# A hybrid decoder layer on one core: three first loads on other queues, and two steps of the output phase moved by one

## The chip, the cores and the metric

The kernel runs on one core of a Trainium2 chip. The metric is the device time of one execution in microseconds; lower is better. A core has TensorE (matrix products; PE in the profile, with its weight loads as PEld), VectorE (DVE), ScalarE (ACT), GpSimd (POOL) and SyncE (SP), each working through its own instruction stream in order, and 16 DMA engines that move data between the memory off the core (HBM) and the core's own. A DMA is issued on the queue of an engine: SP's, ScalarE's or GpSimd's.

## The reference

One layer of a decoder on 256 tokens of width 2048, in float32. The input is normalised, multiplied with one wide matrix, and the columns feed two token mixers side by side: gated linear attention (branch a) and differential attention (branch b). Each branch has an output matrix, the two results are merged by gates, and a last matrix and norm give the output:

```python
h = rmsnorm(x, pre_norm_g[l])
proj = h @ w_in[l]
(a_q, a_k, a_v, a_g, a_lr, b_q, b_k, b_v, b_g, m_a, m_b) = jnp.split(proj, offsets, axis=-1)
...
y_a = o_a @ w_branch_a[l]
...
y_b = o_b @ w_branch_b[l]
merged = jax.nn.sigmoid(m_a) * y_a + jax.nn.sigmoid(m_b) * y_b
out = merged @ w_out[l]
x = x + rmsnorm(out, post_norm_g[l])
```

What matters here is the very first product, `h @ w_in`, which can begin when its first weights, the first part of x and the norm's gains are there; and the end of the chain, where `y_b` is computed in column groups of 512, each group is merged with its part of `y_a`, and the merged values go into `merged @ w_out`.

## The kernel before

**Splits.** Every float32 operand is split in two parts, hi and lo, and a product is the sum of hi x hi, hi x lo and lo x hi. A weight tile of 128 partitions is fetched in `load` (line 284) and split in halves in `emit_half` (line 313): ScalarE copies hi (line 345), VectorE subtracts to get lo (line 346). The hi and lo tiles and the raw tiles have three buffers each. `take` (line 354) hands a split half to the products and emits splits three halves ahead. The sequence of halves, `seq`, is worked out ahead of time, and loads and splits follow it.

**The start.** `preg_s`, the norm's gains (128x16), comes in on ScalarE's queue (line 371). x comes in as 16 blocks of 128x256, turned so that the model dimension lies on partitions: blocks 0 and 1 by the `load_x` of line 372, the others out of `load`, each group after the weight tile that the table `X_LOADS` names. `prep_x` (line 378) multiplies a block by its gain and splits it: hi on ScalarE (line 384), lo on VectorE (line 385). The first weight tile is loaded in two halves (`cuts` in line 294), and its first half is split in two pieces of 416 columns, where hi of the first piece is made by VectorE (line 340) and of the second by ScalarE (line 342). The products of this first stage are those of `first_joint` (lines 516 to 535; they show as L528). Up to then nine products on a tile of ones (line 432) keep TensorE busy.

**The late phase.** Two kinds of work alternate on TensorE, in an order written out by hand in the string `LATE_ORDER`: a point is one step of `late_plain` (line 443), a `p` one step of `half_set` (line 1401). A plain step (`half_tile`, 2.7 us by the profile) is one weight half against both token blocks; steps 0 to 7 are column group 2 of `y_b` ("y12"), steps 8 to 15 group 3 ("y13"), and then products of `w_out` follow. A `p` step is half of one of seven products of a scheme that gets the product of a 2x2 arrangement of blocks with seven multiplications rather than eight; they are taken in the order `LATE = (1, 5, 3, 6, 2, 7, 4)`, two halves each, first for the set "os0" of `w_out`'s columns, then for "os1". Their weights are the fetched blocks and sums of them, tiles `part_e`, `part_b` and `part_f`, formed by accumulating DMAs and by VectorE (line 282). `pinned[0]` is set, so the products stand in program order; the other engines' instructions are ordered by a planner.

After the eighth step of a column group `merged` (line 1324) adds its gate and branch a's part: four VectorE operations on 128x512 (lines 1330 and 1331, twice each), after which a task `turn(g)` is queued that transposes the merged values on TensorE (line 1313) and splits them for the product with `w_out`. `pump` lets such a task go one step after each plain step. The first merge belongs to column group 0, the third to group 2. `put_off` is a list that holds a function to be run later; an earlier phase uses it once and leaves it empty.

Of the kernel before, what the change touches and what calls it, by code (L numbers as in the profile page):

```python
# [36 lines left out]
PUT_OFF = 6  # L37
LATE = (1, 5, 3, 6, 2, 7, 4)
LATE_COLS = ((0, 512), (1536, 1024))
LATE_ORDER = "....." ".p.p.pp.p.pp.p.p.pp.p.pp" ".pp.pp.p.pp.p.p.pp.p.pp"  # L40
BRANCH_COLS = (512, 0)
BRANCH_ORDER = ".p.p.p.p.pp.pp.pp.p.p.p..p"
HALF_SETS = ("ys0", "os0", "os1")
# [67 lines left out]
def half_set_steps(name):  # L111

    steps = []
    for prod in LATE:
        r = {1: 0, 2: 2}.get(prod)
        steps += [("part", name, prod, h) if r is None else (name, r, h) for h in range(2)]
    return steps
# [10 lines left out]
def late_steps():  # L128
# [3 lines left out]
    parts = half_set_steps("os0") + half_set_steps("os1")  # L132
    return [(plain, parts)[n == "p"].pop(0) for n in LATE_ORDER]


@with_exitstack
def hybrid_kernel(ctx: ExitStack, tc, xt, xn, preg, postg, w, w2, gkb, glag, lamv, diffg, ident_d, causal_d, lmask_d, out):
    nc = tc.nc
    pe, act, dve, pool, sp = nc.tensor, nc.scalar, nc.vector, nc.gpsimd, nc.sync
# [12 lines left out]
    def u(shape, name, dtype=F32):  # L152
        count[0] += 1
        return big.tile(shape, dtype, tag="u", name=f"{name}_{count[0]}")
# [24 lines left out]
    def ps(tag):  # L179
        count[0] += 1  # L180
        return psum.tile([P, 512], F32, tag=tag, name=f"{tag}_{count[0]}")
# [28 lines left out]
    def weights(key, r):  # L210
        a, size = at[key][r]
        return w[a : a + P * size].rearrange("(p n) -> p n", p=P), size

    def link(s, name, t):
        count[0] += 1
        c = blocks.tile([P, 2048], F32, tag="chain", name=f"{name}_{count[0]}", bufs=4)
        (pool if s else sp).dma_start(c, weights(f"set{s}", {"a": 0, "b": 6}[name] + t)[0])
        chain[s, name, t] = c
# [65 lines left out]
    def load(j):  # L284
        key, r, h = seq[j]
        src, size = weights(key, r)
        n = size // 2
        early = key == "v0"
        if key == "v3" and r == 0:
            for i in range(2):  # L290
                link(0, "a", i)
        count[0] += 1
        raw = raws[key, r] = wpool.tile([P, 2048], F32, tag="raw", name=f"raw_{count[0]}")
        cuts = (0, n, size) if j in (0, 2) else (0, size)
        for a, b in zip(cuts, cuts[1:]):
            i = sp.dma_start(raw[:, a:b], src[:, a:b])
            if early or key[0] == "o" or key in ("y10", "y11", "y12", "y13", "ys0"):
                tc.keep_in_program_order(i)
        if early and j // 2 in X_LOADS:
            load_x(*X_LOADS[j // 2])  # L300
# [10 lines left out]
    loaded = [0]  # L311

    def emit_half():
# [3 lines left out]
        while loaded[0] < min(j + 2, len(seq)):  # L317
            if len(seq[loaded[0]]) == 3 and seq[loaded[0]][2] == 0:
                load(loaded[0])
            loaded[0] += 1  # L320
# [33 lines left out]
    def take(key):  # L354
        j = used[0]
        used[0] += 1
        while emitted[0] < min(j + 1 + AHEAD, len(seq)):
            emit_half()
        e, hi, lo = ready.pop(j)
        assert key in (e, e[0]), (e, key)  # L360
        return hi, lo
# [3 lines left out]
    preg_s = const.tile([P, KT], F32, name="preg_s")  # L365
    xraw = [u([P, 4, S], "xraw") for _ in range(4)]

    def load_x(kt, n, queue=sp):
        tc.keep_in_program_order(queue.dma_start(xraw[kt // 4][:, kt % 4 : kt % 4 + n, :], xt[:, kt : kt + n, :]))

    tc.keep_in_program_order(act.dma_start(preg_s, preg))
    load_x(0, 2)
    act.preload_act_table_set("natural_log_exp_and_others")

    def x_ops(kt):
# [167 lines left out]
    def half_tile(banks, n, q, ops, hi, lo, begin=0):  # L543
        for w, parts in ((hi, (0, 1)), (lo, (0,))):
            for j in range(2):
                kt = 2 * q + j
                a = ops(kt)
                for b in range(2):
                    for part in parts:
                        first, last = kt == begin and w is hi and part == 0, kt == KT - 1 and w is lo  # L550
                        i = mm(banks[b][:, :n], a[part][:, P * b : P * b + P], w[:, n * j : n * j + n], start=first, stop=last)
        latest[0] = i.ins

    def token_major(key, n, ops, step=1, upto=KT // 2):
        banks = [ps("mm"), ps("mm")]
        for q in range(upto):
            half_tile(banks, n, q, ops, *take(key))
            if q % 2 or not ts:
                pump(step)
            else:  # L560
                pump_eager()
        return banks
# [118 lines left out]
    put_off = []  # L681
# [563 lines left out]
    for g in range(4):  # L1245
        banks = token_major(f"ag{g}", 512, x_ops, LANES)
# [38 lines left out]
    for g in range(4):  # L1285
        parts_a.append(fetch(m0[g], "part", u))
        banks = token_major(f"y0{g}", 512, a_ops, LANES, 4 if g == 3 else 8)
# [14 lines left out]
    def turn(g):  # L1302
        for _ in range({0: 3}.get(g, 2)):
            yield
        copies = u2([P, 4, S], "copy") if g < 2 else None
        if g < 2:
            turned_f32.append(copies)
        for i in range(2):
            bank = ps("bg")
            for j in range(2):  # L1310
                for b in range(2):
                    c = P * (2 * i + j)
                    pe.transpose(bank[:, P * (2 * j + b) : P * (2 * j + b) + P], gb[g][:, b, c : c + P], ident)
            hi = mh[g][:, 2 * i : 2 * i + 2, :].rearrange("p a t -> p (a t)")
            lo = ml[g][:, 2 * i : 2 * i + 2, :].rearrange("p a t -> p (a t)")
            split_out(bank, hi, lo, 0.5)
            if g < 2:
                act.activation(copies[:, 2 * i : 2 * i + 2, :].rearrange("p a t -> p (a t)"), bank, AF.Copy, scale=0.5)
            yield
        done.add(("turn", g))  # L1320
# [3 lines left out]
    def merged(g, banks):  # L1324
        for b in range(2):
            t, src = gb[g][:, b, :], banks[b]
            if g < 2:
                src = ycell(b, g)
                dve.tensor_tensor(out=src, in0=banks[b], in1=src, op=ALU.add if 512 * g == BRANCH_COLS[0] else ALU.subtract)
            dve.scalar_tensor_tensor(out=t, in0=t, scalar=1.0, in1=src, op0=ALU.add, op1=ALU.mult)  # L1330
            dve.tensor_tensor(out=t, in0=t, in1=parts_a[g][:, b, :], op=ALU.add)
        tasks.append(turn(g))
# [3 lines left out]
    def ycell(b, g):  # L1336
        return yc[b][:, 512 * g : 512 * g + 512]
# [20 lines left out]
    def total(b, g, bank, i=None):  # L1358
        t = cell(b, g)
        tc.keep_in_program_order(dve.tensor_tensor(out=t, in0=bank, in1=t, op=ALU.add if left(g) else ALU.subtract))  # L1360
        if i is not None:
            square(b, t, 512, i)
            gain(b, t, 512 * g, 512)
        return t
# [78 lines left out]
    def late_plain():  # L1443
        for g in (2, 3):
            banks = [ps("mm"), ps("mm")]
            for q in range(8):
                half_tile(banks, 512, q, b_ops, *take(f"y1{g}"))
                if q == 7:
                    merged(g, banks)
                yield  # L1450
        pg.extend(u([P, 1024], "pg") for _ in range(2))
        for i in range(2):
            sp.dma_start(pg[i], postg[1024 * i : 1024 * i + 1024].partition_broadcast(P))
        pairs = [[ps("mm"), ps("mm")] for _ in range(2)]
        for r in range(2):
            for g in range(2):
                for h in range(2):
                    half_tile(pairs[g], 512, 4 + 2 * r + h, m_ops, *take(f"o{g}"), begin=8)
                    if r and h:
                        for b in range(2):  # L1460
                            total(b, g, pairs[g][b], g)
                    yield
# [37 lines left out]

    parts = (step for s in range(2) for step in half_set(f"os{s}", m_ops, late, cell, LATE_COLS[s]))
    plain = late_plain()
    pinned[0] = True
    for step in late_steps():
# [124 lines left out]
```

## Time and profile before

| | us |
|---|---|
| median of 3 runs | 1090.54 |
| lowest and highest | 1090.40 and 1091.04 |
| the profiled execution's own time | 1090.65 |
| its span in the profile | 1088.9 |
| granted TensorE clock, mean | 0.999 |
| TensorE's longest waits | 1.6 (before the products on ones), 1.0, 0.9, 0.4 |

The profile is that of one execution, and its span is from the first to the last instruction; 1.75 us of its time lie outside of the span. Times in the rows are counted from the span's start. A row of the timeline gives the start, the duration, the engine, the line, the operation with what it writes and reads, and in brackets the idle time of that engine before it and what ended that. SPq, ACTq and POOLq rows are DMAs being issued; landing is another matter, and the views by tile give it from the issue on. "L540" is the line of a helper through which nearly all products go, so rows are told apart by tile.

### The profile page before, as it was taken

What the parts mean: (1) busy time and instruction counts of PE and PEld (TensorE: products, weight loads), DVE (VectorE), ACT (ScalarE), POOL (GpSimd) and SP (SyncE); (2) the same over time, 40 slices, a digit from 0 to 9 for tenths busy, and PEclk for the clock granted to TensorE, in tenths of its full rate; (3) what the DMA queues carried; (4) which work ended last, traced back from release to release, by engine and by line L of the source; (5) the groups of instructions that cost most, each with busy time, mean ns of one, the idle gap of its engine ahead of it and who ended that gap; (6) DMA issues with size and microseconds to landing.
All of it is one profiled execution on the core that took longest, in us unless ns stands there. A gap on an engine that the chain in (4) does not pass through costs nothing.

```text
span 1088.9 us, 15341 instructions
## 1 busy us (share of the span) xinstructions
PE 1080.3 (99%) x5451; PEld 927.9 (85%) x5451; DVE 917.2 (84%) x1277; ACT 712.2 (65%) x1038; POOL 146.0 (13%) x217
## 2 busy tenths in 40 slices
PE   9999999999999999999999999999999999999997
PEld 8999888888888888888888888889888888888886
DVE  7887987978979889799797999658779867888896
ACT  7886766666666767667666655556777756565662
POOL 0201112021021211211221100020111011100000
PEclk9999999999999999999999999999999999999999
DMA  9889869689798796997986654598888769979752
GB/s 347 294 293 331 237 253 319 163 285 303 263 319 221 278 297 199 331 258 261 300 239 227 238 190 162 184 328 261 275 283 266 275 244 321 345 255 274 262 183 107
DMA packets 63757, 285.06 MB, mean 262 GB/s; under 512 B 8320, under 2 KB 11392, under 8 KB 45504
## 3 DMA queue, kind: packets, MB, share of 16 engines
q1 hardware_dynamic: 39808, 186.87, 48.8%
q0 software_dynamic: 23296, 96.48, 32.7%
q8 instruction: 43, 0.70, 0.2%
q10 hardware_dynamic: 576, 0.73, 0.2%
q14 instruction: 34, 0.28, 0.1%
HBM read 258.88 MB, written 25.17 MB: 261 GB/s over the span
## 4 chain that ended last, share of the span: by engine, by line
PE 98%; issue 1%; DMA 0%; DVE 0%; ACT 0%; POOL 0%; POOLq 0%; SPq 0%; ACTq 0%
PE mm L540 60%; PE bg L540 27%; PE mm L528 2%; PE bg L528 2%; PE mm L513 1%; PE bg L956 1%; PE bg L513 1%; PE bg L1121 0%; PE bg L1095 0%; DMA raw<-in_w_dram 0%; PE bg L1096 0%; PE bg L1133 0%; PE bg L1134 0%; PE bg L1132 0%; PE bg L1016 0%
## 5 line engine op out<-in xcount | busy, mean ns | idle before, releaser
L345 ACT ACTIVATE hi<-raw 128x1024 fp32r<-128x1024 f32 (+3 forms) x261 | 268.1, 1032 | 206.4 <-PE bg L540 103.9
L346 DVE TENSOR_TENSOR lo<-raw,hi 128x1024 fp32r<-128x1024 f32 (+3 forms) x263 | 311.6, 1189 | 87.8 <-ACT hi L345 84.3
L540 PE MATMUL mm<-hi,xs 128*128 128x512 f32 (+1 forms) x848 | 214.1, 386 | 0.0
L540 PEld LDWEIGHTS mm<-hi,xs 128*128 128x128 f32 x848 | 156.9, 188 | 25.9
L540 PE MATMUL bg<-xs,hi 128*128 128x512 f32 x640 | 164.8, 390 | 0.0
L346 DVE TENSOR_TENSOR lo<-a,hi 128x1024 fp32r<-128x1024 f32 x112 | 135.2, 1221 | 11.7 <-ACT hi L345 10.5
L540 PEld LDWEIGHTS bg<-xs,hi 128*128 128x128 f32 x640 | 120.3, 188 | 23.4
L345 ACT ACTIVATE hi<-a 128x1024 fp32r<-128x1024 f32 x112 | 118.6, 1060 | 30.8 <-PE mm L540 22.8
L540 PE MATMUL mm<-lo,xs 128*128 128x512 f32 (+1 forms) x424 | 117.7, 383 | 0.0
L540 PEld LDWEIGHTS bg<-xs,lo 128*128 128x128 f32 x640 | 87.3, 190 | 6.2
L540 PEld LDWEIGHTS mm<-lo,xs 128*128 128x128 f32 x424 | 79.5, 188 | 14.4
L540 PE MATMUL bg<-xs,lo 128*128 128x256 f32 x640 | 89.2, 282 | 0.0
L346 DVE TENSOR_TENSOR lo<-b,hi 128x1024 fp32r<-128x1024 f32 x56 | 67.5, 1224 | 7.8 <-ACT hi L345 6.8
L345 ACT ACTIVATE hi<-b 128x1024 fp32r<-128x1024 f32 x56 | 59.3, 1060 | 18.2 <-PE mm L540 15.8
L540 PE MATMUL mm<-hi,oah 128*128 128x512 f32 x128 | 50.9, 397 | 0.0
L540 PE MATMUL mm<-hi,oal 128*128 128x512 f32 x128 | 50.0, 391 | 0.0
L1107 ACT ACTIVATE prob<-prob,mx,score_scale 128x128 f32<-128x128 f32 x64 | 34.2, 537 | 10.7 <-DVE mx L1102 10.6
L240 POOL DMA_DIRECT2D b<-in_w_dram x28 | 24.4, 873 | 107.4 <-DVE a L248 103.4
L540 PE MATMUL mm<-hi,obh 128*128 128x512 f32 x96 | 37.7, 393 | 0.0
L540 PE MATMUL mm<-hi,obl 128*128 128x512 f32 x96 | 37.4, 390 | 0.0
L345 ACT ACTIVATE hi<-c 128x1024 fp32r<-128x1024 f32 x28 | 29.6, 1060 | 10.2 <-PE mm L540 5.3
L248 DVE TENSOR_TENSOR a<-a,b 128x1024 f32<-128x1024 f32 x28 | 34.1, 1223 | 0.4
(409 smaller groups left out, 2018.6 us busy)
## 6 DMA issues: line engine op xcount, KB each, us to landing
raw<-in_w_dram SPq DMA_DIRECT2D x114, 1024.0 KB, 6.1
a<-in_w_dram POOLq DMA_DIRECT2D x28, 512.0 KB, 13.6
c<-in_w_dram SPq DMA_DIRECT2D x28, 512.0 KB, 8.5
b<-in_w_dram POOLq DMA_DIRECT2D x28, 512.0 KB, 7.3
a<-in_w_dram POOLq DMA_DIRECT2D x12, 1024.0 KB, 5.3
b<-in_w_dram POOLq DMA_DIRECT2D x12, 1024.0 KB, 8.2
raw<-in_w_dram SPq DMA_DIRECT2D x14, 832.0 KB, 6.9
dh<-dh POOLq DMA_DIRECT2D x16, 256.0 KB, 4.7
```

Of the source, the lines that this page charges most:

```text
L240: pool.dma_start(chain[s, name, i][:, c], weights(f"set{s}", 2 + i)[0][:, c], accum_op=ALU.add)
L248: dve.tensor_tensor(out=a, in0=a, in1=chain[s, "b", i][:, c] if second else raws[s, i, h], op=ALU.add)
L345: act.activation(hi_t[:, a:b], r[:, a:b], AF.Copy)
L346: dve.tensor_tensor(out=lo_t[:, a:b], in0=r[:, a:b], in1=f32(hi_t[:, a:b]), op=ALU.subtract)
L513: i = pe.matmul(out, lhs, rhs, start=first and n == 0, stop=last and n == len(pairs) - 1, **kw)
L528: i = pe.matmul(banks[g][b][:, :n], a[part][:, P * b : P * b + P], w[:, n * g : n * g + n], start=first, stop=last)
L540: i = pe.matmul(*args, **kw)
L956: pe.matmul(o, xk[:, P * c : P * c + P], xq.rearrange("p (b c t) -> p b c t", b=2, c=4)[:, :, c, :], start=i == 0, stop=i == 1)
L1107: act.activation(prob[m][:, lo:up], prob[m][:, lo:up], AF.Exp, scale=score_scale[:, b : b + 1], bias=mx[:, i : i + 1], accum_out=z[:, i : ...
```

## The change

Four edits. The gains `preg_s` are loaded on GpSimd's queue. The first weight tile is loaded right behind the first blocks of x and ahead of the load of ScalarE's function table; its first half goes on ScalarE's queue, its second half, as all other weights, on SP's. In the late order the two halves of product 1 of "os0" each stand one plain step further ahead: before, the string read `......p.p.pp`, now `.....p.p..pp`, and from there on it is as it was. And the third merge, that of group 2, is not emitted after the last step of "y12" but kept in `put_off` and emitted after the first step of "y13", with its task `turn(2)`.

```diff
-LATE_ORDER = "....." ".p.p.pp.p.pp.p.p.pp.p.pp" ".pp.pp.p.pp.p.p.pp.p.pp"
+LATE_ORDER = ".....p.p..pp.p.pp.p.p.pp.p.pp" ".pp.pp.p.pp.p.p.pp.p.pp"
...
-            i = sp.dma_start(raw[:, a:b], src[:, a:b])
+            i = (sp if j or a else act).dma_start(raw[:, a:b], src[:, a:b])
...
-    tc.keep_in_program_order(act.dma_start(preg_s, preg))
+    tc.keep_in_program_order(pool.dma_start(preg_s, preg))
     load_x(0, 2)
+    load(0)
+    loaded[0] += 1
     act.preload_act_table_set("natural_log_exp_and_others")
...
                 half_tile(banks, 512, q, b_ops, *take(f"y1{g}"))
-                if q == 7:
+                if put_off and q == 0:
+                    put_off.pop()()
+                if q == 7 and g == 2:
+                    put_off.append(lambda banks=banks: merged(2, banks))
+                elif q == 7:
                     merged(g, banks)
                 yield
```

## The prediction

> **What bounds the kernel now.** I read the first page of the profile, then TensorE's waits over the whole span, then the two places where those waits fall: the first 6 us and the stretch around 984 us.
>
> ```profile
> span 1088.9 us, 15341 instructions
> PE 1080.3 (99%) x5451; PEld 927.9 (85%) x5451; DVE 917.2 (84%) x1277; ACT 712.2 (65%) x1038; POOL 146.0 (13%) x217
> PE 98%; issue 1%; DMA 0%; DVE 0%; ACT 0%; POOL 0%; POOLq 0%; SPq 0%; ACTq 0%
> PE bg L1567 <- ACT diag L1566: 1.0, 1, 1.0
> PE mm L528 <- ACT hi L342: 0.9, 1, 0.9
> PE bg L540 <- DVE lo L346: 0.4, 1, 0.4
> ```
>
> TensorE is busy for 99% of the span and is 98% of the chain that ended last. The last three rows are its waits (engine, line and releaser, then total us, times, longest). Only three matter: the last step of the output (1.0 us), the first real product (0.9) and one product in the output phase (0.4). The change adds no matmul and removes none, so its worth is what it does to the second and third wait, plus any wait that it makes. The first is in the tail, which it leaves alone.
>
> The start, as the timeline has it (start, duration, engine, line), with the piece of the chain before it and the landing times of two tiles, `preg_s` first and `xraw` second:
>
> ```profile
> 0.74 0.41 ACTq L371 DMA_DIRECT2D preg_s<-in_preg_dram  x1
> 0.74 0.39 SPq L369 DMA_DIRECT2D xraw<-in_xt_dram  x1
> 4.63 0.51 ACT L384 ACTIVATE xs<-xraw,preg_s 128x256 fp32r<-128x256 f32 x1 [2.17 <-DMA preg_s<-in_preg_dram]
> 5.17 0.48 DVE L385 SCALAR_TENSOR_TENSOR xs<-xraw,preg_s,xs 128x256 fp32r<-128x256 f32 x1 [3.63 <-ACT xs L384]
> 5.47 0.55 ACT L342 ACTIVATE hi<-raw 128x416 fp32r<-128x416 f32 x1 [0.34 <-DMA raw<-in_w_dram]
> 5.57 0.37 DVE L340 CAST hi<-raw 128x416 fp32r<-128x416 f32 x1
> 6.08 0.98 PE L528 MATMUL mm<-hi,xs 128*128 128x416 f32 x4 [0.92 <-ACT hi L342]
> ...
> 1.19 4.27 DMA raw<-in_w_dram
> ...
> DMA to landing us min/median/max: 3.9/3.9/3.9
> ...
> DMA to landing us min/median/max: 3.7/7.2/9.3
> ```
>
> Three things must land before the first product: the norm's weights (0.74 + 3.9 = 4.63), the first two blocks of x (0.74 + 3.7 = 4.44) and the first half tile of weights (1.19 + 4.27 = 5.46). Behind them run two paths of almost one length. ScalarE's ends at 5.47 + 0.55 = 6.02, set by the weights. VectorE's goes over the split of x: 4.63, 5.17, then the cast at 5.57, which ends at 5.94. So bringing the weights sooner, alone, is worth 0.08 us; the other path then holds the first product. It has a fixed length of 6.08 - 4.63 = 1.45 us from the moment when x and the norm's weights are both there.
>
> What the DMA engines do meanwhile (stretch, then busy time of each engine, granted clock, DMA share, GB/s), and the packets of SP's queue (q1) and ScalarE's (q10): up to 2.0 us, from 2.0 to 2.7, from 2.7 to 3.4, and q10's from 2.0 to 4.2 us:
>
> ```profile
> 2.00:3.00 1.00, 1.00 (x4) 0.45 (x3) 0.00 (x0) 0.46 (x1) 0.00 (x0) 1.00 0.94 192
> 4.20:5.20 1.00, 0.97 (x4) 0.20 (x2) 0.03 (x1) 0.51 (x1) 0.00 (x0) 1.00 0.96 366
> ...
> q1 hardware_dynamic: 18, 0.04, 7.1%
> ...
> q1 hardware_dynamic: 73, 0.15, 102.9%
> q10 hardware_dynamic: 59, 0.00, 5.6%
> ...
> q1 hardware_dynamic: 61, 0.13, 67.7%
> q10 hardware_dynamic: 63, 0.00, 6.0%
> ...
> q10 hardware_dynamic: 144, 0.01, 4.3%
> ```
>
> From 2 us on the 16 engines are full, at shares of 0.94 and 0.96. And the two queues take turns: the 144 small packets of the norm's weights, 8 KB in all, need 2.2 us, because they go in step with SP's (59 beside 73, 63 beside 61).
>
> **The change part by part: the start.** It moves three issues. The first half tile goes to ScalarE's queue at 0.74 instead of 1.19, and SP's later issues move up by about the same 0.45. The norm's weights go to GpSimd, ahead of the clearing of a 128x1024 tile (0.95 us, the first row of the fence below) that only later loads of constants need. The act-table load keeps its place: ScalarE has issued one DMA ahead of it in either kernel.
>
> If nothing else moved, the half tile would be there at 0.74 + 4.27 = 5.01, x at 4.44, and the first product at 4.44 + 1.45 = 5.89: 0.19 us sooner, not 0.45, because the path over x decides. That is the best end.
>
> Against it stands the turn taking. The half tile now competes with x. Of x (256 KB, 128 packets) all but 18 packets are still to come at 2.0 us, 7 of 8 on an engine. If each of the 7 lets one 3.25 KB packet of weights go first, at 366 GB/s over 16 engines (0.15 us each), x is late by 7 x 0.15 = 1.0 us, less the small packets that leave ScalarE's queue. That is the worst end: 1.0 later. The bytes ahead of the first product are the same, and the engines were full already; only their order changes, and the order of before (x first) was the right one for the longer path. Between -0.19 and +1.0 I take the middle, **+0.4 us**: nothing shows at which packet of x the weights join.
>
> The Trainium skill says the same against this move: "DMA: Bandwidth & Descriptors", section "Issuing engines are not separate DMA queues", has it that transfers issued from several engines run on the same 16 DMA engines and save only the issue time. By that rule the sum of the start would be zero at most, and the shares of 0.94 and 0.96 agree.
>
> For the norm's weights on GpSimd's queue, before has no such small transfer. The nearest rows are its spills of 256 KB (issue, then landing times of `dh`):
>
> ```profile
> 0.73 0.95 POOL L408 MEMSET w_raw<- 128x1024 f32 x1 [0.29 <-POOLq L1622]
> L171 POOL DMA_DIRECT2D dh<-dh x16: 539/576/588, 323.4 to 782.0; - x16
> DMA to landing us min/median/max: 2.3/5.7/11.1
> ```
>
> From 0.73 the bounds are 3.0 (the fastest spill, on a quiet queue) and 11.8 (the slowest, queued behind others). Nothing is queued on GpSimd at 0.73, so I take the low side with the turn taking of its own 3.9 us: landing at 4.6 to 5.0, no later than x in the forecast, so it adds nothing. Both ends stay for the range.
>
> A figure of the skill, same page, section "Latency and other measured facts", puts a software queue's first byte at about 1 us against 0.6; by it the sum would be 0.4 later where these weights are last. No run here shows it for a small transfer.
>
> After the first product the shift carries through to the end one for one, since TensorE waits nowhere between 6.1 and 984 us.
>
> **The late steps.** Here products are cut into short halves (rows marked bg) between longer ones (mm). The rows, first of TensorE, then VectorE and ScalarE:
>
> ```profile
> 977.42 0.39 PE L540 MATMUL bg<-hi,r1h 128*128 128x512 f32 x1
> 978.78 0.39 PE L540 MATMUL bg<-hi,r1h 128*128 128x512 f32 x1
> 982.86 0.39 PE L540 MATMUL bg<-hi,s4h 128*128 128x512 f32 x1
> 984.34 0.73 PE L540 MATMUL bg<-lo,s4h 128*128 128x512 f32 x2 [0.41 <-DVE lo L346]
> 984.91 0.39 PE L540 MATMUL mm<-hi,obh 128*128 128x512 f32 x1
> 986.74 1.07 PE L540 MATMUL mm<-lo,obh 128*128 128x512 f32 x4
> ...
> 978.53 1.06 ACT L345 ACTIVATE hi<-part_b 128x1024 fp32r<-128x1024 f32 x1 [0.75 <-PE bg L540]
> ...
> 977.79 0.68 DVE L1330 SCALAR_TENSOR_TENSOR gateb<-gateb,mm 128x512 f32<-128x512 f32 x1
> 980.66 0.69 DVE L1331 TENSOR_TENSOR gateb<-gateb,part 128x512 f32<-128x512 f32 x1
> 981.26 0.68 DVE L1330 SCALAR_TENSOR_TENSOR gateb<-gateb,mm 128x512 f32<-128x512 f32 x1
> 982.46 0.69 DVE L1331 TENSOR_TENSOR gateb<-gateb,part 128x512 f32<-128x512 f32 x1
> 983.06 1.22 DVE L346 TENSOR_TENSOR lo<-part_b,hi 128x1024 fp32r<-128x1024 f32 x1
> 984.20 1.22 DVE L346 TENSOR_TENSOR lo<-raw,hi 128x1024 fp32r<-128x1024 f32 x1
> ```
>
> A short half takes 978.78 - 977.42 = 1.36 us undisturbed; the one at 982.86 took 984.91 - 982.86 = 2.05. So the wait costs 0.69 us, more than the 0.41 of its row. Its cause: the low part of `part_b` could be made from 978.53 + 1.06 = 979.59 on and is needed at about 983.8, but VectorE came to it at 983.06, behind the four operations of the third merge (0.68 + 0.69 + 0.68 + 0.69 = 2.74 us).
>
> With the merge emitted one long step later, those 2.74 us no longer stand ahead of that low part: it ends near 982, and the wait goes. What is late next? The low part for the following long product, at 984.20 in before, with all four operations already done, ends at 985.42. Its use at 986.74 moves up to 986.05. So even if all of the merge falls ahead of it, 0.6 us are left. The merge's result is not pressing: its transposes go one long step later, and the output products that read them come only after all eight long steps of the next tile. The first product's step forward reads what the first merge left, two merges back, and a weight tile that is loaded in the same order as before; no instruction or DMA is added by it, and I cost it at nothing. **-0.7 us.**
>
> **The sum.** +0.4 - 0.7 = -0.3 us, against this execution's 1090.65; the median of the runs shown is 1090.54, so I forecast **1090.2 us**. A difference of 0.2% (2.2 us) is about what a measurement of this kernel can tell from no change, so this counts as the same.
>
> **The rivals.** (1) As forecast: x and weights share the engines, the late wait goes; 1089.9 to 1090.7. Chance 0.48.
> (2) x is not delayed: start -0.19, late -0.69, so 1089.7. For it: x has a lead of 18 packets, and its packets are the shorter ones. Against it: the turn taking above. Chance 0.22. The skill's same page, section "Queues, rings and completion order", would give this case: an engine is said to drain a whole packet of some 9 to 17 descriptors from one queue before it turns to the next. The even counts of the two queues in the rows speak against it.
> (3) The planner puts the merge's operations where they hold another low part, or moves nothing: the late wait stays, in this place or another. Start +0.4, late 0: 1090.9, with 0.7 more if the moved wait is dearer: 1091.6. For it: none of VectorE's rows above has idle time ahead of it, so whatever moves there pushes something. Chance 0.17.
> (4) The other side: the norm's weights land late on GpSimd's queue, and the split of x waits for them. Each microsecond behind 4.63 is one microsecond at the end; the kernel is slower than before once they come after 5.3 us (4.63 + 0.69) and slower by over 0.2% after 7.5. At the median landing of the spills, 0.73 + 5.7 = 6.4, the sum is +1.8 - 0.7 = +1.1: 1091.6; at 8 us it would be +2.7: 1093.2. For it: spreads of 2.3 to 11.1 us on that queue. Against it: the long ones stood behind other transfers. Chance 0.13.
>
> **Range and chances.** Low: case 2 and 0.4 of scatter, 1089.3. High: the middle of case 4 and the dear end of case 3, 1092.0. Left out are the late end of case 4 and what the planner may do elsewhere. Faster by over 0.2% would need 2.2 us, and all that waits outside the tail is 0.9 + 0.7: 0.01. Slower by over 0.2%: the late half of case 4, 0.06. The same: 0.93.
>
> **What would show it.** In the changed profile TensorE's first product at 6.3 to 6.7 us, with the split of x starting near 5.0 and x (not the half tile) landing later than 3.7 us; TensorE's wait list without the row of 0.4 us; the merge's four operations behind the low part of `part_b`. The half tile landing near 5 us and the first product still after 6 would confirm that the path over x decides. A first product before 5.9, a new row of TensorE's waits between 10 and 1070 us, or the norm's weights landing after 5.3 us would make the prediction wrong.

## The result: 0.3% slower, and the profile after

| | before | after |
|---|---|---|
| median of 9 runs each, us | 1090.79 | 1094.48 |
| lowest and highest, us | 1090.28 and 1093.27 | 1093.51 and 1094.83 |
| ratio of the times, 95% interval | | 1.0032 [1.0023, 1.0041] |
| the profiled execution's own time, us | 1090.65 | 1093.58 |
| its span, us | 1088.9 | 1091.7 |

The forecast was 1090.2 with a range up to 1092.0, so the change is slower than the range allows.

The page of after opens with its span and its busy times:

```profile
span 1091.7 us, 15340 instructions
PE 1082.0 (99%) x5451; PEld 929.3 (85%) x5451; DVE 916.7 (84%) x1277; ACT 711.4 (65%) x1038; POOL 146.7 (13%) x218
```

TensorE's products are the same 5451, but it is busy for 1.7 us more (1080.3 before). So a part of the loss isn't waiting: some products ran slower. The waits of TensorE in after are three (engine, line and releaser; total us, times, longest):

```profile
PE mm L530 <- ACT xs L386: 2.3, 1, 2.3
PE bg L434 <- DVE ones_b L431: 1.6, 1, 1.6
PE bg L1573 <- ACT diag L1572: 1.0, 1, 1.0
```

The row of 0.4 us in the output phase is gone, as forecast. The wait ahead of the first real product went from 0.9 to 2.3 us, and its releaser is no longer the weights (`hi`) but the split of x (`xs`). The timeline of the start (start, duration) shows why:

```profile
0.74 0.41 ACTq L296 DMA_DIRECT2D raw<-in_w_dram  x1
0.74 0.39 SPq L369 DMA_DIRECT2D xraw<-in_xt_dram  x1
...
1.18 0.42 SPq L296 DMA_DIRECT2D raw<-in_w_dram  x1
...
1.26 0.71 POOL L371 DMA_DIRECT2D preg_s<-in_preg_dram  x1 [0.81 <-POOLq L1628]
...
6.37 0.51 ACT L386 ACTIVATE xs<-xraw,preg_s 128x256 fp32r<-128x256 f32 x1 [3.90 <-DMA preg_s<-in_preg_dram]
...
7.31 0.37 DVE L340 CAST hi<-raw 128x416 fp32r<-128x416 f32 x1
...
7.83 1.04 PE L530 MATMUL mm<-hi,xs 128*128 128x416 f32 x4 [2.34 <-ACT xs L386]
```

The split of x starts at 6.37, released by the gains `preg_s`. The view of DMA issues (size, then us from issue to landing) has x, SP's second transfer (the other half of the first weight tile), the half tile on ScalarE's queue and the gains:

```profile
xraw<-in_xt_dram SPq DMA_DIRECT2D x1, 256.0 KB, 4.3
...
raw<-in_w_dram SPq DMA_DIRECT2D x1, 416.0 KB, 5.0
...
raw<-in_w_dram ACTq DMA_DIRECT2D x1, 416.0 KB, 4.5
...
preg_s<-in_preg_dram POOLq DMA_DIRECT2D x1, 8.0 KB, 5.1
```

From the issue times above, x landed at 0.74 + 4.3 = 5.04, the half tile at 5.24, SP's second transfer at 1.18 + 5.0 = 6.18, and the gains, 8 KB, last of all at 1.26 + 5.1 = 6.36. From there the path over x takes 7.83 - 6.37 = 1.46 us, the 1.45 of before. The first product is 7.83 - 6.08 = 1.75 us late.

The second loss stands in the stretches behind it (stretch, length, busy time and products of TensorE, of its weight loads, VectorE, ScalarE and GpSimd, granted clock, DMA share, GB/s). After:

```profile
5.20:8.60 3.40, 1.06 (x5) 0.80 (x5) 1.69 (x4) 2.23 (x6) 0.00 (x0) 1.00 1.04 407
8.60:12.00 3.40, 3.40 (x12) 3.28 (x11) 3.40 (x8) 3.24 (x6) 0.00 (x0) 0.51 1.02 418
12.00:15.40 3.40, 3.40 (x19) 3.37 (x19) 2.58 (x4) 0.94 (x2) 0.00 (x0) 0.99 1.02 416
```

The same view of before:

```profile
5.20:8.60 3.40, 2.52 (x13) 2.54 (x14) 3.37 (x8) 2.74 (x6) 0.00 (x0) 1.00 1.02 356
8.60:12.00 3.40, 3.40 (x19) 3.36 (x19) 3.00 (x5) 2.71 (x4) 0.00 (x0) 1.00 1.01 400
```

In after TensorE is busy for 31% of the stretch up to 8.60 (1.06 of 3.40), and then its granted clock is 0.51 for 3.4 us: 12 products in place of 19, with TensorE busy all the time.

Setting the start of every product beside that of the same product of before gives the account: +1.75 at the first product; +3.30 by 15 us, so **+1.55** while the clock was halved; +0.19 at 567 us; **-0.70** in the output phase; and 2.8 at the end, as the spans say (1091.7 - 1088.9). At 567 us the products themselves have no wait row, but the weight loads have one that before lacks there, for the low part of a split:

```profile
PEld mm L542 <- DVE lo L346: 0.3, 1, 0.3
```

The late steps did what was said. VectorE's timeline in after:

```profile
985.70 1.21 DVE L346 TENSOR_TENSOR lo<-part_b,hi 128x1024 fp32r<-128x1024 f32 x1
...
987.97 0.68 DVE L1332 SCALAR_TENSOR_TENSOR gateb<-gateb,mm 128x512 f32<-128x512 f32 x1
...
989.70 0.68 DVE L1333 TENSOR_TENSOR gateb<-gateb,part 128x512 f32<-128x512 f32 x1
```

The low part of `part_b` now comes first, the merge's operations behind it.

### The profile page after: what moved, and what is told of

The parts are those of the page before. It is cut to its first block, busy times and chain, and to the rows that moved or that the text cites. A ratio compares the mean times of both kernels' runs of the same rounds, so it can differ in the third digit from the quotient of the medians.

```text
span 1091.7 us, 15340 instructions
## 1 busy us (share of the span) xinstructions
PE 1082.0 (99%) x5451; PEld 929.3 (85%) x5451; DVE 916.7 (84%) x1277; ACT 711.4 (65%) x1038; POOL 146.7 (13%) x218
## 4 chain that ended last, share of the span: by engine, by line
PE 98%; issue 1%; DMA 0%; ACT 0%; POOL 0%; DVE 0%; POOLq 0%; ACTq 0%
PE mm L542 60%; PE bg L542 27%; PE mm L530 2%; PE bg L530 2%; PE mm L515 1%; PE bg L958 1%; PE bg L515 1%; PE bg L1123 0%; DMA preg_s<-in_preg_dram 0%; PE bg L1097 0%; PE bg L1098 0%; PE bg L1135 0%; PE bg L1136 0%; PE bg L1134 0%; PE bg L1018 0%
## 5 line engine op out<-in xcount | busy, mean ns | idle before, releaser
L346 DVE TENSOR_TENSOR lo<-raw,hi 128x1024 fp32r<-128x1024 f32 (+3 forms) x263 | 310.9, 1187 | 88.7 <-ACT hi L345 85.4
L542 PE MATMUL mm<-hi,xs 128*128 128x512 f32 (+1 forms) x848 | 214.1, 386 | 0.0
L542 PEld LDWEIGHTS mm<-hi,xs 128*128 128x128 f32 x848 | 156.8, 188 | 26.0
L542 PE MATMUL bg<-xs,hi 128*128 128x512 f32 x640 | 164.8, 389 | 0.0
L346 DVE TENSOR_TENSOR lo<-a,hi 128x1024 fp32r<-128x1024 f32 x112 | 135.0, 1219 | 11.9 <-ACT hi L345 10.5
L542 PEld LDWEIGHTS bg<-xs,hi 128*128 128x128 f32 x640 | 120.3, 188 | 23.4
L542 PE MATMUL mm<-lo,xs 128*128 128x512 f32 (+1 forms) x424 | 117.9, 384 | 0.0
L542 PEld LDWEIGHTS bg<-xs,lo 128*128 128x128 f32 x640 | 87.3, 190 | 6.2
L542 PEld LDWEIGHTS mm<-lo,xs 128*128 128x128 f32 x424 | 79.4, 188 | 14.7 <-DVE lo L346 0.3
L542 PE MATMUL bg<-xs,lo 128*128 128x256 f32 x640 | 89.2, 282 | 0.0
L346 DVE TENSOR_TENSOR lo<-b,hi 128x1024 fp32r<-128x1024 f32 x56 | 67.4, 1220 | 7.8 <-ACT hi L345 6.8
L542 PE MATMUL mm<-hi,oah 128*128 128x512 f32 x128 | 50.8, 397 | 0.0
L542 PE MATMUL mm<-hi,oal 128*128 128x512 f32 x128 | 50.0, 391 | 0.0
L542 PE MATMUL mm<-hi,obh 128*128 128x512 f32 x96 | 37.7, 392 | 0.0
L542 PE MATMUL mm<-hi,obl 128*128 128x512 f32 x96 | 37.4, 390 | 0.0
```

The source lines that it names most:

```text
L346: dve.tensor_tensor(out=lo_t[:, a:b], in0=r[:, a:b], in1=f32(hi_t[:, a:b]), op=ALU.subtract)
L542: i = pe.matmul(*args, **kw)
```

## The experiments

Three theories were tried against each other. **Gains:** they land late, because GpSimd's load is served behind something. **Weights:** the half tile on ScalarE's queue delays what the first product needs. **Clock:** TensorE's longer wait halves its clock, and that is a loss of its own. The shifts given below are those of TensorE's products against the same products of before.

### The two ends of the change, each alone

`late_only` is before with the two late edits (the order and the third merge), `start_only` before with the three issues moved:

```diff
 late_only:
+LATE_ORDER = ".....p.p..pp.p.pp.p.p.pp.p.pp" ".pp.pp.p.pp.p.p.pp.p.pp"
...
+                if put_off and q == 0:
+                    put_off.pop()()
+                if q == 7 and g == 2:
+                    put_off.append(lambda banks=banks: merged(2, banks))
...
 start_only:
+            i = (sp if j or a else act).dma_start(raw[:, a:b], src[:, a:b])
...
+    tc.keep_in_program_order(pool.dma_start(preg_s, preg))
     load_x(0, 2)
+    load(0)
+    loaded[0] += 1
```

> The late edits alone: the moved product of os0 and the third merge, with the start as before. If the late steps do what the prediction said, the wait of 0.4 us on the low part of part_b is gone and the time is 0.6 to 0.7 us under before. If the slowdown hides in the late steps (a new wait), it is at or above before.

> The three start edits alone, the late phase as before. If all of the slowdown is made in the first 12 us: first product near 7.8 us, granted clock 0.5 for 3.4 us behind it, and 3.3 to 4.4 us above before. If the late edits share in it: less than 3.

Measured: `late_only` 1089.98 us, ratio 0.9991 [0.9983, 1.0]; `start_only` 1094.58, ratio 1.0033 [1.002, 1.0045]. The whole loss is in the start. The late edits alone have the lowest median of this study, with an interval that reaches 1.0. In `late_only`'s profile the row of 0.4 us is gone and the output phase is 0.54 us shorter. In `start_only`'s the row stands, `PE bg L542 <- DVE lo L346: 0.4, 1, 0.4`, the first product comes at 8.09, and the clock rose late; this stretch shows how late:

```profile
8.60:12.00 3.40, 3.40 (x11) 3.25 (x10) 3.40 (x7) 2.56 (x5) 0.00 (x0) 1.00 1.01 412
```

Eleven products in 3.40 us are half speed. The clock column says 1.00 here because the trace has no record of the clock ahead of its first change, which came at 13.98: **ahead of the first record, the products per stretch tell the clock, the column doesn't.** At 14 us the shift is +4.7, so this profiled execution (1095.97, the highest of five) lost 2.7 us by the clock on top of 2.0 by waiting.

### The gains alone on GpSimd, with the clearing moved, and an unread load there

`gains_pool` moves only the gains. `no_clear` is after with GpSimd's clearing of a 128x1024 tile, which stands behind the load, given to VectorE. `touch` is before with one more 8 KB load on GpSimd that nothing reads.

```diff
 gains_pool:
-    tc.keep_in_program_order(act.dma_start(preg_s, preg))
+    tc.keep_in_program_order(pool.dma_start(preg_s, preg))
 no_clear:
-    pool.memset(w2_tile[0], 0.0)
+    dve.memset(w2_tile[0], 0.0)
 touch:
+    spare = const.tile([P, KT], F32, name="spare")
+    tc.keep_in_program_order(pool.dma_start(spare, preg))
```

> The kernel before with the norm's gains alone moved to GpSimd's queue; weights and x stay on SP's. If the gains' landing is the whole cause: they land some 5.1 us after issue at 1.26, first product near 7.8 us, a stretch of half clock, 2.5 to 4.5 us above before. If the moved weights matter as much: first product near 6.5, about 1 us above before.

> The changed kernel with the clearing of the 128x1024 tile on VectorE rather than on GpSimd behind the gains' load. If that clearing holds up the gains' descriptors: gains land 2.5 to 3 us sooner, at 3.5 to 4 us, first product near 6.5. If the first DMA of GpSimd's queue is late by itself: gains still land at 6 to 6.7 us, first product near 7.8.

> The kernel before with one more load on GpSimd's queue at the start, of the same 8 KB into a tile that nobody reads. If the first DMA of that queue pays a start-up of some 2.7 us: this load lands near 5 us after its issue, and the first spill (44.9 us, first packet after 3.8 us in before) now starts 1.1 to 1.3 us after its issue. If each transfer is late by what stands beside it: the spill still needs 3.8 us. The time is that of before either way.

Measured: `gains_pool` 1093.22, ratio 1.0019 [1.001, 1.0028]; `no_clear` 1093.32, ratio 1.0032 [1.0019, 1.0046]; `touch` 1090.68, ratio 1.0001 [0.9992, 1.001]. So the unread load costs nothing, the clearing isn't the cause (the gains land at 6.45 without it), and this one line, the gains on GpSimd, makes the kernel 2.5 us slower by itself. Nor is it a start-up that the queue pays once: in `touch` the first spill behind the unread load has its first packet 4.2 us after its issue (3.8 for that spill in before), while a spill at 67.4 us of before needs 1.1. The DMA rows of `gains_pool` (SP's issues at 0.74 and 1.19, GpSimd's at 1.25):

```profile
xraw<-in_xt_dram SPq DMA_DIRECT2D x1, 256.0 KB, 3.5
...
raw<-in_w_dram SPq DMA_DIRECT2D x1, 416.0 KB, 4.1
preg_s<-in_preg_dram POOLq DMA_DIRECT2D x1, 8.0 KB, 4.2
```

The gains land at 1.25 + 4.2 = 5.45, a whole microsecond behind x (0.74 + 3.5 = 4.24), and just behind SP's second transfer (1.19 + 4.1 = 5.29). The first product is 0.88 us late (6.96), between the two expectations. And here too the clock fell:

```profile
4.50:7.92 3.42, 1.59 (x8) 1.08 (x7) 1.84 (x5) 2.42 (x6) 0.00 (x0) 1.00 1.01 366
7.92:11.33 3.41, 3.41 (x12) 3.22 (x11) 3.41 (x8) 2.90 (x6) 0.00 (x0) 0.50 1.04 424
11.33:14.74 3.41, 3.41 (x20) 3.37 (x19) 2.37 (x4) 1.27 (x2) 0.00 (x0) 1.00 1.02 421
```

46% busy, then 3.41 us at half clock, 12 products, then 20. That costs 1.57 us, and 0.88 + 1.57 = 2.45 is this profile's loss by 15 us. The ten executions lie in two groups, four from 1091.57 to 1092.37 and six from 1093.19 to 1093.76, with a gap that fits the halved stretch, though only one has a trace; the profiled one (1093.26) is in the upper group.

### What the gains wait for

`held` puts the gains on GpSimd and makes SP's first weight load wait for a clearing of its tile, so that little is queued on SP when GpSimd's load is issued:

```diff
+        if j == 0:
+            dve.memset(raw, 0.0)
...
-    tc.keep_in_program_order(act.dma_start(preg_s, preg))
+    tc.keep_in_program_order(pool.dma_start(preg_s, preg))
```

> The kernel before with the gains on GpSimd's queue, and a clearing of the first weight tile on VectorE, for which SyncE's first weight load has to wait: it is then issued some 2 us later, and only x of SyncE's transfers is queued when GpSimd's load is issued at 1.25 us. Theory (GpSimd's transfer is served when an engine is done with what SyncE had queued ahead of it, the first half tile in the run of the gains alone, where it landed at 5.47 us): the gains now land with x or right behind it, at 3.0 to 4.6 us. Rival (GpSimd's first transfer takes about 3 to 4 us to its first packet whatever else is queued): 5.3 to 5.6 us again or, by the 2.9 us of the unread load, 4.4 to 5. Between 4.4 and 4.6 it tells nothing. The first products themselves come later than before, by the held load: 7 to 9 us.

Measured in one execution: 1100.56 us. Both theories missed with their numbers, for a reason that helps: with the first weights held, a load of a later stage, of 1 MB, went ahead on SP's queue (issued at 1.18). The rows, with GpSimd's issue at 1.24:

```profile
xraw<-in_xt_dram SPq DMA_DIRECT2D x1, 256.0 KB, 3.6
...
a<-in_w_dram SPq DMA_DIRECT2D x1, 1024.0 KB, 5.8
preg_s<-in_preg_dram POOLq DMA_DIRECT2D x1, 8.0 KB, 5.9
```

SP's second transfer is now 1 MB and lands at 6.98; the gains land at 7.14, although x had landed at 4.33. Set side by side (landing = issue + time to landing of the rows of each run):

| run | SP's second transfer landed | GpSimd's 8 KB landed |
|---|---|---|
| gains_pool | 5.29 | 5.45 |
| touch (the unread load) | 5.59 | 5.85 |
| no_clear | 6.29 | 6.45 |
| after | 6.18 | 6.36 |
| start_only | 6.38 | 6.66 |
| warm_more (below) | 6.48 | 6.66 |
| held | 6.98 | 7.14 |

In seven runs GpSimd's load lands 0.2 to 0.3 us behind SP's second transfer, wherever that is, while x is there 1.2 to 2.8 us before. The packets say the same. The first of GpSimd's went out at 4.07 us in `gains_pool`, when SP had moved 0.6 of the 0.69 MB of its first two transfers, and at 5.68 in `held`, at 1.2 of 1.31 MB. A fixed time of GpSimd's own to its first packet is excluded: from the issue it took 2.8 us in the one and 4.4 in the other. So the gains don't take turns with SP's transfers packet by packet, as they did on ScalarE's queue in before; they come out with the end of the transfer that SP queued beside them. No run here shows by which rule they miss the gap between x and that transfer.

The Trainium skill, "DMA: Bandwidth & Descriptors", section "Queues, rings and completion order", says that an engine drains a packet of some 9 to 17 descriptors from one queue before it goes on to the next. For GpSimd against SP the table agrees in so far as a whole transfer of SP's, of 416 KB or 1 MB, passes first. For ScalarE against SP the prediction's rows of before speak against it: there 59 packets stood beside 73.

### The weights' move without the gains'

`gains_back` is after with the gains back at the head of ScalarE's queue, the half tile behind them. `x_halved` has the late edits and, at the start, block 0 of x alone first and block 1 behind the first half tile, all on SP.

```diff
 gains_back (against after):
-    tc.keep_in_program_order(pool.dma_start(preg_s, preg))
+    tc.keep_in_program_order(act.dma_start(preg_s, preg))
 x_halved (against late_only):
+            if j == 0 and a == 0:
+                load_x(1, 1)
...
-    load_x(0, 2)
+    load_x(0, 1)
```

> The changed kernel with the norm's gains back on ScalarE's queue, ahead of the half tile of weights. If the gains' way over GpSimd is the cause: first product at 6.2 to 6.6 us (x lands some 0.6 us later than in before, since the weights take turns with it), no half clock, and the time is 0.7 under to equal to before. If the moved weights are the cause: still 2 us or more above before.

> The late edits, and at the start block 0 of x alone ahead of the first half tile of weights, block 1 behind it, all on SP's queue, gains on ScalarE's. If bytes ahead of the first product decide: 128 KB fewer at some 260 GB/s, first product 0.3 to 0.5 us sooner (5.6 to 5.8), time 0.9 to 1.1 under before. If issue and landing decide: first product at 6.0 as in before, 0.6 under before.

Measured: `gains_back` 1092.67, ratio 1.001 [1.0001, 1.0019]; `x_halved` 1090.67, ratio 0.9999 [0.999, 1.0007]. In `gains_back` the split of x starts at 4.19, as the landings of x (0.74 + 3.2) and the gains (0.74 + 3.4) allow. But the weights are late. Both halves of the tile are issued at 1.18, and the DMA rows give their landing, ScalarE's first:

```profile
raw<-in_w_dram ACTq DMA_DIRECT2D x1, 416.0 KB, 5.5
raw<-in_w_dram SPq DMA_DIRECT2D x1, 416.0 KB, 5.3
```

The timeline shows what waits for them:

```profile
6.73 0.55 ACT L342 ACTIVATE hi<-raw 128x416 fp32r<-128x416 f32 x1 [2.03 <-DMA raw<-in_w_dram]
...
7.33 0.64 PE L530 MATMUL bg<-hi,xs 128*128 128x416 f32 x2 [1.72 <-ACT hi L342]
```

The half that is needed first now lands last, at 6.68, in step with the one that isn't needed yet (6.48), and the first product is 1.25 us late, at 7.33. So the weights on ScalarE's queue lose by another road too: two queues share 16 engines that were full, and the needed transfer is the loser. It isn't the change's own case, since there the half tile is issued at 0.74 and lands at 5.24. The executions lie in two groups here too (1090.69 to 1091.67, with the profiled one, and 1092.55 to 1093.48). Both expectations missed: the kernel is neither back at before nor 2 us above it. Beside `late_only`, which has the same late edits, the weights' move costs 2.7 us by the medians (1092.67 and 1089.98), about as much as the gains' move alone (2.5).

`x_halved` shows the reverse. Its first product comes at 5.13, 0.96 us sooner than in before and sooner than either expectation, and by 9 us nothing is left of it. TensorE didn't wait for anything behind that product; it ran at half speed:

```profile
5.13 1.87 PE L530 MATMUL mm<-hi,xs 128*128 128x416 f32 x4
...
4.17:7.58 3.41, 3.41 (x11) 2.62 (x10) 1.87 (x5) 0.95 (x2) 0.00 (x0) 1.00 0.87 277
```

The same four products took 0.98 us in before, and the clock's first record, a rise, came at 7.58 rather than 4.58. So in this profile the lead went to the clock. The next weights came later too (their split starts at 7.69, in before at 6.67), but no product waited for them; what they would have cost at full clock no run shows.

### The clock

`warm_more` is after with 21 instead of 9 warm-up products on ones, to fill TensorE's wait; `warm11` is `late_only` with 11.

```diff
 warm_more:
-WARM = 9
+WARM = 21
 warm11:
-WARM = 9
+WARM = 11
```

> The changed kernel with 21 products on the tile of ones at the start rather than 9, so that TensorE stays busy until the gains land. If the half clock comes from TensorE's 2.3 us without work: first product still near 7.8 us, granted clock 1.0 from 5 us on, some 1.5 us faster than the changed kernel, about 1 to 2 us above before. If the half clock has another cause: the same time as the changed kernel.

> The two late edits with the start as before, and 11 warm-up products instead of 9. Theory (TensorE's clock rises at the end of a stretch of some 3.4 us that it nearly filled; two more warm-up products fill it from about 1 us to the first real product at 6.1 us, so that the rise comes early in more of the executions): 1089.4 to 1090.2, against 1090.7 to 1090.8 before and 1089.98 with the late edits alone, and fewer executions at 1092 or more. Rival (the warm-up's length does nothing for the clock, or the two products delay the first real ones): 1090.0 to 1090.8, the scatter as before.

Measured: `warm_more` 1093.81, ratio 1.0026 [1.0017, 1.0034]; `warm11` 1090.34, ratio 0.9995 [0.9986, 1.0004]. In `warm_more`'s profile the clock stays full from 5.89 us on, although the first product comes at 8.12, later than in after: the halving goes when TensorE's wait is filled. By the median it lies between its two expectations, 0.7 us under after. What the clock saves can't be read from its time, because the longer warm-up made the kernel's planner order the first stages otherwise, and a new wait at 50 to 60 us (1.4 us in the shift) took its place:

```profile
PEld mm L542 <- ACT hi L345: 1.3, 3, 0.7
```

The same new wait stands in `no_clear`, where the planner's order of the first stages differs too. Its start, though, is a clean case: +1.89 at the first product and +1.90 at 42 us, with the clock full. VectorE clears first there, so the products on ones begin 1.1 us later, and TensorE's wait for the gains is 1.4 us in place of 2.3. `warm11` did not become faster: in its profile the clock rose at 7.64 (`late_only`: 6.92), and the whole is within the scatter of `late_only`.

### The two late edits

`merge_only` puts off the third merge and leaves the order; `order_only` moves the output's first product and leaves the merge.

```diff
 merge_only:
+                if put_off and q == 0:
+                    put_off.pop()()
+                if q == 7 and g == 2:
+                    put_off.append(lambda banks=banks: merged(2, banks))
...
 order_only:
+LATE_ORDER = ".....p.p..pp.p.pp.p.p.pp.p.pp" ".pp.pp.p.pp.p.p.pp.p.pp"
```

> The put-off third merge alone, without the step of the output's first product. Theory (the merge is the working edit, since what waited was the evicting of a bank behind the four merge operations on VectorE): the wait of 0.41 us at the second halves of the output's products is gone, the late phase is 0.5 to 0.7 us shorter as with both late edits (0.54), the whole 1090.0 to 1090.4 against 1090.7 to 1090.8 before. Rival (the step of the output's product is the working one): the wait stays, the time is that of before.

> The output's first product a step forward alone, the third merge where it was. Theory (the merge is the working edit): the wait of about 0.4 us stays or grows by up to one merge operation (to 0.8), the late phase is 0 to 0.4 us longer than before, the whole 1090.7 to 1091.2. Rival (this is the working one): the wait goes, 1090.0 to 1090.4.

Measured: `merge_only` 1090.42, ratio 0.9998 [0.9989, 1.0006], with the row of 0.4 gone and the output phase 0.70 us shorter in its profile, though its median isn't clear of the noise; `order_only` 1092.28, ratio 1.0015 [1.0006, 1.0024]. The merge is the working edit; what waited was a low part, as the row says, not the evicting of a bank. The step of the output's product, alone, does harm, and more than expected: 1.5 us by the medians, and in the profiled execution (1093.99, the highest of eleven) the output phase is 3.0 us longer, not up to 0.4. Its waits there show the first half of why:

```profile
PE bg L540 <- DVE lo L346: 0.8, 1, 0.8
PE bg L540 <- ACT p L1426: 0.7, 1, 0.7
```

The stretches at the same place show the second half:

```profile
983.07:986.49 3.42, 1.86 (x8) 1.03 (x7) 3.42 (x6) 1.29 (x3) 0.00 (x0) 1.00 0.87 169
986.49:989.90 3.41, 3.41 (x10) 2.64 (x9) 3.38 (x4) 0.70 (x1) 0.00 (x0) 0.50 0.54 143
```

Two waits, 1.5 us together, leave TensorE busy for 54% of a stretch, and the next 3.41 us run at half clock: 10 products, where before did 16 in that stretch. It is the start's loss again, a thousand microseconds later, and neither wait is for a DMA.

## Why the prediction was wrong, step by step

- **Start, x against the weights (+0.4, x to land at 5.0):** x landed at 5.04, as said; since +0.4 was the middle of two bounds, that is in part luck. With the gains there in time this would have put the first product at 5.04 + 1.45 = 6.5, inside the forecast 6.3 to 6.7. It was covered by the gains, so no run shows the term alone. What was missed is that the half tile can be the loser as well (first product +1.25 in `gains_back`).
- **Gains on GpSimd, "landing at 4.6 to 5.0, no later than x in the forecast, so it adds nothing": this step failed.** They landed at 6.36. The two mistakes in it: the load was put at 0.73, where the clearing had been, and issued at 1.26; and it was taken to share turns with SP as ScalarE's queue does, while it came in behind the end of SP's second transfer. The weights' move, priced for x alone, makes that transfer land at 6.18 in place of 5.29 (`gains_pool`), so the two edits of the start hurt each other.
- **The price of rival 4, one microsecond for one:** right for the wait (landing 1.73 behind 4.63, first product 1.75 late), but not the whole price. That its 6.4 met the measured 6.36 is luck: it counts the median of 256 KB spills, 5.7, from 0.73, and the 8 KB took 5.1 from 1.26. Its 1091.6 lacks 1.55 us for the halved clock; 1091.6 + 1.55 + 0.19 at 567 us = 1093.34, beside 1093.58 in the profiled execution. The prediction had no term for the clock; that alone put the upper end of the range, 1092.0, too low. The case itself had a chance of 0.13, and one line of the change was enough for it.
- **Late steps (-0.7):** right in size and cause. -0.70 in after and with the merge alone, -0.54 in `late_only`. The margin was smaller than said: the low part of `part_b` was to end near 982 and ended at 986.91, which less after's shift of 3.51 is 983.4, ahead of a use at about 983.8. "I cost it at nothing" for the order's step holds only with the merge put off; alone it costs 1.5 us by the medians and 3.0 in its profile.
- **The rest of the list of signs:** of the signs named for a wrong forecast one was there, the gains after 5.3; the first product came at 7.83, not at 6.3 to 6.7. Rival 2 (x not delayed) fell with x at 5.04; rival 3 fell with the wait's row gone.
- **Open:** why the low part at 567 us came later; why GpSimd's load isn't served between x and SP's second transfer; and why the median lost more (3.7) than the profiled execution (2.9). `start_only`'s profile shows the likely reason, a clock that rises later still, but after itself has one profile.

## What to carry to other kernels

A small transfer that everything waits for belongs at the head of a queue whose transfers take turns at once; here that was ScalarE's, and on GpSimd's queue 8 KB came in behind 416 KB, and once behind 1 MB. With 16 DMA engines full, a move to another queue changes only which transfer loses: name that one before making the move. And price a wait of TensorE that covers about half of some 3.4 us at twice its length or more, because the stretch behind it can run at half clock.

## What the runs showed of the hardware

**The clock goes down after short waits.** It changed in steps of 3.41 us. It fell behind stretches in which TensorE was busy for 13% (`held`, at 51 us), 31% (after, one wait of 2.3 us), 46% (`gains_pool`, 1.8) and 54% (`order_only`, 0.8 and 0.7). It stayed behind one of `no_clear` with 59%, and behind this one of `gains_back`, with 55%:

```profile
2.38:5.79 3.41, 3.23 (x8) 0.91 (x6) 0.48 (x1) 1.07 (x2) 0.00 (x0) 1.00 1.01 329
5.79:9.20 3.41, 1.87 (x10) 1.86 (x11) 2.26 (x5) 2.47 (x6) 0.00 (x0) 1.00 1.03 398
```

The first row, 95% busy, is the one at whose end the clock rose there. The Trainium skill, "TensorE: Matmul & The Clock Gate", section "Part 1: The HAM clock gate (the "warmup" mystery)", has the same 3413 ns, free-running. It puts the fall behind an idle window of about 3.4 us; here 0.8 and 0.7 us of waiting, in one window, were enough.

**The clock's rise scatters from run to run, and with it the time.** In the fourteen profiles it first rose between 4.5 and 14 us. The stretches at whose end it rose were at least 85% busy; in the profile of `touch` one of 81% (first row; the first product had come at 6.27, nearly as in before) did not do, and the clock rose only at 10.93:

```profile
4.10:7.50 3.40, 2.75 (x8) 1.51 (x7) 2.11 (x5) 2.12 (x5) 0.00 (x0) 1.00 1.00 373
7.52:10.93 3.41, 3.41 (x12) 3.25 (x11) 3.02 (x7) 2.90 (x6) 0.00 (x0) 1.00 1.05 416
10.93:14.34 3.41, 3.41 (x20) 3.37 (x18) 2.15 (x4) 1.76 (x3) 0.00 (x0) 1.00 1.02 419
```

That execution took 1092.97 us, and the other nine 1090.23 to 1090.93. So a change of the start is measured against a scatter of 1 to 3 us, and only many executions show which way it moved the odds.
